# HGRN2 inside a hybrid trunk step: forward queries with backward keys in one tile, forward keys with backward queries in another, scaled over all 128 rows, with a PSUM bank and a mask per direction

## The chip, the cores and the metric

The kernel runs on one core of a Trainium2 chip. The metric is the device time of one execution in microseconds (us); lower is better. A profile of one execution lists each engine's instructions: PE (TensorE matmuls; PEld its weight loads), DVE (VectorE), ACT (ScalarE), POOL (GpSimd), and SP (SyncE, which issues most DMAs).

## What is computed

One inference step of a trunk of two layers over 640 tokens: 512 latent tokens (four tiles of 128, numbers 0 to 3) and 128 prompt tokens (tile 4). In each layer a modulation, one input projection, three token mixers side by side (differential attention, gated DeltaNet, HGRN2), one output projection, a layer norm and a SwiGLU feed-forward part. The change touches HGRN2, which has 4 heads of 64 keys and 64 values and scans the tokens in both directions:

```
def hgrn_mixer(q_raw, f_raw, i_raw, gate, lb, norm_g, s0):
    q = silu(q_raw)                                   # one set of queries for both directions
    v = i_raw
    forget = lbb + (1.0 - lbb) * sigmoid(f_raw)       # per direction, token, head and key
    key = 1.0 - forget
    g = log(forget)
    o_f, s_f = gla_chunked(q, key[0], v, g[0], s0[:, 0])
    o_b, s_b = gla_chunked(_flip(q), _flip(key[1]), _flip(v), _flip(g[1]), s0[:, 1])
    o = o_f + _flip(o_b)
    return rms_norm(o, norm_g) * silu(gate), [s_f, s_b]
```

`gla_chunked` is gated linear attention in pieces of the sequence (b is the cumulated sum of g inside a piece):

```
    dec = jnp.where(causal, jnp.exp(b_t - b_s), 0.0)
    attn = jnp.einsum('bhntsd,bhnsd->bhnts', q * dec, k)
    intra = jnp.einsum('bhnts,bhnse->bhnte', attn, v)
    o = intra_n + jnp.einsum('bhcd,bhde->bhce', q_n * jnp.exp(b), S)
    S = S * jnp.exp(b_last) + jnp.einsum('bhcd,bhce->bhde', k_n * jnp.exp(b_last - b), v_n)
```

So token t reads key s at or before it with the weight of q_t on key_s times the product of the forgets after s up to t, and the state that came in.

## The kernel before

Tokens are kept with the 64 keys of a head on the partitions: rows 0 to 63 belong to the forward direction, rows 64 to 127 to the backward one, and a tile is 128 rows x 4 heads x 128 tokens. `hgrn_local` makes the weights inside a tile by levels instead of by divisions of cumulated products. At level n (1, 2, 4, ... 64) the tile's tokens stand in pairs of blocks of n. A query in the later block of a pair (for the backward direction, the earlier one) reads the keys in the other block; its own product of forgets since its block's border is already multiplied into it, and into the keys the product up to the border. After a level, queries of the later blocks and keys of the earlier ones are multiplied by the whole product over the other block, which the tile `T` (names hT) holds for each block and which is itself halved by a product of neighbours (`Tn`).

The names and lines: `q5` (hq) holds the queries of all five tiles, loaded twice, into rows 0 to 63 and 64 to 127; `f5` (hf) the forgets of both directions; `Kr` (hK) a tile's keys of both directions. The local function `diag` makes 8 matmuls for a tile (4 heads, 2 halves of 64 tokens), each over all 128 rows, so that both directions are summed in one bank (names ph{level}_{layer}_{tile}). So that each direction brings only its own pairs, ACT first copies the half of the queries that may read (`A.copy`, L623) into a tile `Qm` (hqm) whose other positions POOL set to zero at the stage's start (L1443; nine tiles in layer 0, eight in layer 1). DVE takes the level's new weights out of the bank into `aD` (haD) where the level's mask is set (L624, `copy_predicated`); the mask hmask has 64 columns for each of six levels. Then DVE scales the queries and POOL the keys, two operations each, one for every direction's 64 rows (L176 is the line of the helper `tt` that issues all of them), and POOL makes Tn. At level 64 there are 8 matmuls of 64x64 without a mask. `key_T` transposes the keys (phk, hkn); pha are the tile's sums of keys and values, pho the outputs, pth their transposition into `xT`.

The PSUM banks are given out by classes: during this stage the class "h" of HGRN has three banks, P2, P2b and R2, which it takes in turn; "as" and "pt_po" belong to attention, "m" to the modulation.

What runs beside it: `open_h` (L1432) starts HGRN together with the modulation matmuls (`mods`, names psm) and with the output of DeltaNet; attention runs through the same time, one block per head and query tile (pas_{layer}_{head}_{tile} scores, anm, ae softmax, pat, pao, ao, asm, pto). Python generators are taken in turns (`run` with TURNS), and a scheduler sets the order in which each engine gets its instructions. After the stage the output projection (pop) fills PE. The mask and the attention's lambda (dl) are loaded at the program's start through SP's queue.

Of the kernel before, what the change touches and what calls it, by code (L numbers as in the profile page):

```python
# [10 lines left out]
F32 = mybir.dt.float32  # L11
# [34 lines left out]

NQ2 = (3, 2)
LATE = (2, 2)
# [6 lines left out]
def _const_arrays():  # L55
# [41 lines left out]
    for k, a in parts.items():  # L97
# [3 lines left out]
        cols.append(a)  # L101
    m = [((rc // (2 * b)) == (tc // (2 * b))) & ((rc // b) != (tc // b)) for b in (1, 2, 4, 8, 16, 32)]
    _CONST["f"] = np.concatenate(cols, 1)
# [6 lines left out]
def tile_trunk(  # L110
# [269 lines left out]

    hmask = cp.tile([P, 6 * 64], U8, name="hmask")
    hmf = cp.tile([P, 6 * 64], F32, tag="dl", name="hmf")
    S.dma_start(hmf, constm)
    V.tensor_copy(hmask, hmf)

# [192 lines left out]

    def hgrn_local(l, taus, hp, st, hqm, f5):
        X = {}  # L580
        q5 = hp.tile([P, 4, NTOK], F32, name=f"hq{l}")
        v5 = hp.tile([P, NT, 256], F32, name=f"hv{l}")
        for d in range(2):
            ds_ = slice(64 * d, 64 * d + 64)
            S.dma_start(q5[ds_], cqs[l].rearrange("(h j) t -> j h t", j=64))
        S.dma_start(v5, cis[l].rearrange("(t p) c -> p t c", p=P))
        for tau in taus:
            tsl = slice(tau * P, (tau + 1) * P)
            n_ = f"{l}_{tau}"
            q, f, v = q5[:, :, tsl], f5[:, :, tsl], v5[:, tau]  # L590
            Kr = hp.tile([P, 4, P], F32, tag="hK", bufs=NT, name=f"hK{n_}")
            T = hp.tile([P, 4, P], F32, tag="hT", bufs=NT, name=f"hT{n_}")
            aD = hp.tile([P, 4, 64], F32, tag="haD", bufs=NT, name=f"haD{n_}")
            X[tau] = dict(q=q, f=f, v=v, Q=q, K=Kr, T=T, aD=aD, Tv=f, To=0)

        def diag(x, rhs, nm):
            ps = psS("h", nm)
            pv = ps[:, :256].rearrange("p (h t) -> p h t", t=64)
            for h in range(4):
                for c_ in range(2):  # L600
                    cs = slice(64 * c_, 64 * c_ + 64)
                    mm(pv[cs, h, :], x["K"][:, h, cs], rhs[:, h, cs])
            return pv

        for tau in taus:
            x = X[tau]
            V.tensor_scalar(x["K"], x["f"], -1.0, 1.0, ALU.mult, ALU.add)
            tt(V, x["aD"], diag(x, x["q"], f"ph0_{l}_{tau}"), bc(K("identc"), 1, 4), ALU.mult)
            tt(G, x["Q"], x["q"], x["f"], ALU.mult)
        yield  # L610
        for i, n in enumerate((1, 2, 4, 8, 16, 32, 64)):
            nb = P // (2 * n)
            for tau in taus:
                x = X[tau]
                Q, Kr, T, Tv = x["Q"], x["K"], x["T"], x["Tv"]

                def half(ap, d, u):
                    return ap[64 * d:64 * d + 64].rearrange("p h (b u n) -> p h b u n", u=2, n=n)[:, :, :, u, :]

                if n < 64:  # L620
                    Qm = hqm[i][tau % len(hqm[i])]
                    for d in range(2):
                        A.copy(half(Qm, d, 1 - d), half(Q, d, 1 - d))  # L623
                    V.copy_predicated(x["aD"], bc(hmask[:, i * 64:(i + 1) * 64], 1, 4),  # L624
                                      diag(x, Qm, f"ph{n}_{l}_{tau}"))
                else:
                    aT = x["f"]
                    x["aT"] = aT
                    ps = psS("h", f"ph{n}_{l}_{tau}")
                    po = ps[:, :256].rearrange("p (h t) -> p h t", t=64)  # L630
                    for h in range(4):
                        for c_ in range(2):
                            cs, co = slice(64 * c_, 64 * c_ + 64), slice(64 - 64 * c_, 128 - 64 * c_)
                            mm(po[cs, h, :], Kr[cs, h, cs], Q[cs, h, co])
                    for c_ in range(2):
                        cs, co = slice(64 * c_, 64 * c_ + 64), slice(64 - 64 * c_, 128 - 64 * c_)
                        A.copy(aT[cs, :, cs], x["aD"][cs])
                        A.copy(aT[cs, :, co], po[cs])
                for d in range(2):
                    up, lo = 1 - d, d  # L640

                    def tb(u):
                        y = Tv[64 * d:64 * d + 64].rearrange("p h (b u) -> p h b u", u=2)[:, :, :, u]
                        return y.unsqueeze(3).to_broadcast([64, 4, nb, n])
# [4 lines left out]
                Tp = Tv.rearrange("p h (b u) -> p h b u", u=2)  # L649
                tt(G, Tn, Tp[:, :, :, 0], Tp[:, :, :, 1], ALU.mult)  # L650
                x["Tv"], x["To"] = Tn, x["To"] + nb
            yield

        def key_T(tau):
            ps = psS("h", f"phk{l}_{tau}")
            pk = ps.rearrange("p (j t) -> p j t", t=P)
            for h in range(4):
                nc.tensor.transpose(pk[:, h, :], X[tau]["K"][:, h, :], ident)
            kn = hp.tile([P, 4, P], F32, tag="hkn", bufs=2, name=f"hkn{l}_{tau}")
            A.copy(kn, pk)  # L660
            return kn

        kn = key_T(taus[0])
        for i, tau in enumerate(taus):
            x, nxt = X[tau], key_T(taus[i + 1]) if i + 1 < len(taus) else None
            ps = psS("h", f"pha{l}_{tau}")
            pa = ps[:, :256].rearrange("p (h v) -> p h v", v=64)
            for h in range(4):
                mm(pa[:, h, :], kn[:, h, :], x["v"][:, h * 64:h * 64 + 64])
            Ab = x["T"][:, :, 0:64]  # L670
            A.copy(Ab, pa)
            st[tau] = (x["Q"], x["Tv"][:, :, 0], Ab, x["aT"], x["v"])
            kn = nxt
# [15 lines left out]

    def hgrn(l, hp, hqm, xT, f5):  # L690
        ready = []
# [22 lines left out]

        yield from hgrn_local(l, list(range(NT)), hp, st, hqm, f5)
        for d in range(2):
# [628 lines left out]
    for l in range(DEPTH):  # L1345
# [86 lines left out]
        def open_h(rest):  # L1432
# [13 lines left out]
            return [(mods(), TURNS[l][3]), (hgrn(l, hp, hqm, xT, held["f5"]), TURNS[l][4]), (delta_T(), 1)]  # L1446

# [323 lines left out]
```

## Time and profile before

| | |
|---|---|
| median of 3 runs | 2097.5 us (2095.54 to 2103.86) |
| the profiled execution | 2094.8 us, span 2093.0 us |
| mean granted clock | 0.956 |
| busy, share of the span | PE 91%, PEld 80%, DVE 69%, ACT 38%, POOL 42% |
| HGRN levels, layer 0 | 379.5 to about 480 us |
| HGRN levels, layer 1 | about 1410 to 1510 us |

Shares of the span are means over stages with different limits. A row of a group of instructions gives its busy time, the mean of one, and the engine's idle time just before it with what ended it. The clock is TensorE's, in parts of full speed.

### The profile page before, as it was taken

The numbers are of one execution on the slowest core, as the hardware profiler recorded it, in microseconds if no ns is written. First come the engines' busy times: TensorE is split into PE (matmuls) and PEld (weight loads), VectorE is DVE, ScalarE is ACT, GpSimd is POOL, SyncE is SP. The second block draws the span as 40 slices with busy tenths as digits, with TensorE's granted clock in tenths as the row PEclk, the third lists the DMA queues.
The fourth block names the chain that finished last, engine by engine and source line by source line (L and its number), as shares of the span: only waits on it lengthen the run. The fifth ranks groups of instructions, "written<-read, shape, count | busy, mean of one in ns | idle before, by whom it ended". The sixth has DMA issues, their size and how long they took to land.

```text
span 2093.0 us, 37831 instructions
## 1 busy us (share of the span) xinstructions
PE 1912.6 (91%) x14914; PEld 1676.2 (80%) x14914; DVE 1439.1 (69%) x2516; ACT 792.7 (38%) x1564; POOL 883.5 (42%) x988
## 2 busy tenths in 40 slices
PE   7999997888978999999989999978889789999996
PEld 5988986667758989989989879755677779989895
DVE  5458524897488867667666774359847897667676
ACT  3542322666143334323345323146742434334231
POOL 0375235775042132444246814358632311432445
PEclk7999998898999999999999999989899899999998
DMA  8423225865453323222433331386344233223221
GB/s 282 132 77 122 90 68 140 218 195 196 146 164 94 109 81 101 68 84 76 127 121 109 123 116 56 101 192 201 125 158 135 83 109 91 71 81 101 71 77 75
DMA packets 243400, 249.36 MB, mean 119 GB/s; under 512 B 19371, under 2 KB 190359, under 8 KB 243223
## 3 DMA queue, kind: packets, MB, share of 16 engines
q1 hardware_dynamic: 240630, 245.11, 38.4%
q8 instruction: 118, 1.93, 0.4%
q10 hardware_dynamic: 2592, 1.84, 0.3%
q14 instruction: 60, 0.48, 0.1%
HBM read 218.72 MB, written 28.18 MB: 118 GB/s over the span
## 4 chain that ended last, share of the span: by engine, by line
PE 26%; DVE 10%; POOL 5%; DMA 3%; issue 3%; ACT 2%; SPq 1%; POOLq 0%; ACTq 0%; DVEq 0%
PE pfo L173 6%; PE pfd L173 3%; PE pfc L173 3%; PE pfa L173 3%; PE pop L173 3%; PE pfb L173 1%; PE pci L173 1%; DVE hl L176 1%; DVE hq L176 1%; PE pcf L173 1%; POOL r L176 1%; PE pbq L173 1%; PE ph L173 1%; DVE fs L176 1%; DMA avf<-vsc 1%
## 5 line engine op out<-in xcount | busy, mean ns | idle before, releaser
L176 DVE TENSOR_TENSOR hl<-raw,hl 128x1024 fp32r<-128x1024 f32 (+1 forms) x210 | 279.6, 1335 | 92.1 <-ACT hl L273 74.2
L173 PE MATMUL pfo<-hl,ha 128*128 128x512 f32 x1320 | 312.8, 395 | 1.6 <-ACT hl L273 0.8
L173 PEld LDWEIGHTS pfo<-hl,ha 128*128 128x128 f32 x1320 | 246.1, 187 | 60.6 <-DVE ha L176 1.6
L176 POOL TENSOR_TENSOR r<-r,ft 128x512 f32<-128x512 f32 x96 | 142.8, 1506 | 245.2 <-DVE ft L176 244.4
L176 POOL TENSOR_TENSOR t<-raw 128x512 f32<-128x512 f32 x44 | 65.7, 1493 | 336.6 <-DMA raw<-in_w_ffn_in_dram 168.3
L273 ACT CAST hl<-raw 128x1024 fp32r<-128x1024 f32 (+2 forms) x122 | 125.9, 1036 | 152.4 <-DMA raw<-in_w_ffn_out_dram 47.8
L173 PE MATMUL pfc<-sx,hl 128*128 128x320 f32 x1056 | 173.4, 312 | 9.8 <-ACT hl L1550 7.2
L173 PE MATMUL pfa<-xT,hl 128*128 128x320 f32 x1056 | 172.7, 313 | 4.7 <-DVE hl L176 3.0
L173 PEld LDWEIGHTS pfc<-sx,hl 128*128 128x128 f32 x1056 | 161.5, 190 | 13.5 <-ACT hl L1550 7.8
L1550 ACT CAST hl<-raw 128x1024 fp32r<-128x1024 f32 x88 | 92.0, 1051 | 204.4 <-PE pfo L173 105.7
L173 PEld LDWEIGHTS pfa<-xT,hl 128*128 128x128 f32 x1056 | 161.0, 191 | 8.0 <-DVE hl L176 3.8
L173 PE MATMUL paq<-xT,hl 128*128 128x320 f32 x768 | 123.8, 318 | 1.4 <-ACT az L1238 1.4
L173 PE MATMUL pop<-hl,xT 128*128 128x512 f32 x480 | 122.4, 407 | 0.0
L173 PEld LDWEIGHTS paq<-xT,hl 128*128 128x128 f32 x768 | 116.1, 191 | 4.5 <-ACT az L1238 2.1
L173 PEld LDWEIGHTS pop<-hl,xT 128*128 128x128 f32 x480 | 89.5, 193 | 25.2 <-issue 6.8
L176 DVE TENSOR_TENSOR ft<-pfo,lg 128x512 f32<-128x512 f32 x96 | 63.8, 683 | 54.6 <-PE pfo L173 44.1
L176 POOL TENSOR_TENSOR hK<-hK,hT 64x256 f32<-64x256 f32 x120 | 87.6, 730 | 29.9 <-PE ph L173 23.2
L176 DVE TENSOR_TENSOR t<-raw,t 128x512 f32<-128x512 f32 x88 | 73.9, 840 | 35.7 <-POOL t L176 35.6
L173 PE MATMUL pfd<-xT,h 128*128 128x320 f32 x528 | 85.2, 310 | 10.0 <-DVE u L176 10.0
L173 PE MATMUL pbq<-xT,hl 128*128 128x320 f32 x576 | 89.7, 312 | 1.0 <-DVE hl L176 0.4
L173 PE MATMUL pfb<-sx,hl 128*128 128x320 f32 x528 | 88.7, 310 | 0.6 <-DVE hl L176 0.6
L173 PEld LDWEIGHTS pfd<-xT,h 128*128 128x128 f32 x528 | 79.0, 188 | 11.6 <-issue 8.9
(409 smaller groups left out, 4206.1 us busy)
## 6 DMA issues: line engine op xcount, KB each, us to landing
raw<-in_w_ffn_in_dram SPq DMA_DIRECT2D x96, 512.0 KB
raw<-in_w_mod_dram SPq DMA_DIRECT2D x80, 512.0 KB
raw<-in_w_in_dram SPq DMA_DIRECT2D x56, 512.0 KB
raw<-in_w_ffn_out_dram SPq DMA_DIRECT2D x44, 512.0 KB
pc<-in_w_mod_dram SPq DMA_DIRECT2D x8, 1024.0 KB
raw<-in_w_out_dram SPq DMA_DIRECT2D x16, 512.0 KB
qksc<-az SPq DMA_DIRECT2D x16, 320.0 KB
qkhi<-azs SPq DMA_DIRECT2D x16, 256.0 KB
```

Source lines behind the costliest of these rows:

```text
L173: nc.tensor.matmul(out, lhsT, rhs, start=start, stop=stop, **kw)
L176: return eng.tensor_tensor(out, a, b, op)
L273: A.copy(hl[:, 0, :kt * n], raw[:, :kt * n])
L1550: A.copy(tile_[:, 0, :n], raw)
```

## The change

The queries and keys of a direction no longer stand in tiles of their own kind. `x5` (hx) holds the forward queries in rows 0 to 63 and the backward keys in rows 64 to 127; `y5` (hy) the forward keys and the backward queries. Of a pair of blocks the later one is scaled in x for both directions (forward queries, backward keys) and the earlier one in y, so each is one operation over 128 rows. x is scaled by DVE for even tiles and by POOL for odd ones, y always by POOL. The loads of queries go from two to three. Level 0 still uses a tile with both directions' keys (`kt`, names hk0), from which ACT copies the two halves into their places; the queries' first product is two POOL operations of 64 rows.

At levels 1 to 32 each direction has a bank of its own: 16 matmuls of 64x64 for a tile, two `copy_predicated` with a mask for each direction (12 masks of 64 columns, loaded in three parts through the buffer of dl). Qm, its copies and memsets go. `key_T` transposes x and y, copies the half of each that holds keys, and then puts the backward queries beside the forward ones.

```diff
-        for d in range(2):
-            S.dma_start(q5[ds_], cqs[l].rearrange("(h j) t -> j h t", j=64))
+        for sl, t5 in ((LO, x5), (HI, x5), (HI, y5)):
+            S.dma_start(t5[sl], cqs[l].rearrange("(h j) t -> j h t", j=64))
...
-            V.tensor_scalar(x["K"], x["f"], -1.0, 1.0, ALU.mult, ALU.add)
-            tt(V, x["aD"], diag(x, x["q"], f"ph0_{l}_{tau}"), bc(K("identc"), 1, 4), ALU.mult)
-            tt(G, x["Q"], x["q"], x["f"], ALU.mult)
+            kt = hp.tile([P, 4, P], F32, tag="hk0", bufs=2, name=f"hk0{l}_{tau}")
+            V.tensor_scalar(kt, f, -1.0, 1.0, ALU.mult, ALU.add)
...
+                    mm(pv[cs, h, :], kt[:, h, cs], x["x"][:, h, cs])
+            for k, sl in ((kf, LO), (kb, HI)):
+                A.copy(k, kt[sl])
+            tt(V, x["aD"], pv, bc(K("identc"), 1, 4), ALU.mult)
+            for q, sl in ((qf, LO), (qb, HI)):
+                tt(G, q, q, f[sl], ALU.mult)
...
                 if n < 64:
-                    Qm = hqm[i][tau % len(hqm[i])]
+                    pv = [psS("h", f"ph{n}_{d}_{l}_{tau}")[:, :256].rearrange("p (h t) -> p h t", t=64) for d in range(2)]
+                    for h, d, c_, cs in chunks():
+                        k, q = x["kq"][d]
+                        mm(pv[d][cs, h, :], k[:, h, cs], q[:, h, cs])
                     for d in range(2):
-                        A.copy(half(Qm, d, 1 - d), half(Q, d, 1 - d))
-                    V.copy_predicated(x["aD"], bc(hmask[:, i * 64:(i + 1) * 64], 1, 4),
-                                      diag(x, Qm, f"ph{n}_{l}_{tau}"))
+                        V.copy_predicated(x["aD"], bc(hmask[:, (2 * i + d) * 64:(2 * i + d + 1) * 64], 1, 4), pv[d])
...
-                for d in range(2):
-                    up, lo = 1 - d, d
...
-                    tt(V, half(Q, d, up), half(Q, d, up), tb(lo), ALU.mult)
-                    tt(G, half(Kr, d, lo), half(Kr, d, lo), tb(up), ALU.mult)
+                def scaled(eng, ap, u):
+                    y = ap.rearrange("p h (b u n) -> p h b u n", u=2, n=n)[:, :, :, u, :]
+                    tt(eng, y, y, Tp[:, :, :, 1 - u].unsqueeze(3).to_broadcast([P, 4, nb, n]), ALU.mult)
+
+                scaled(G if tau % 2 else V, x["x"], 1)
+                scaled(G, x["y"], 0)
...
+            for src, sl in ((x["y"], LO), (x["x"], HI)):
+                pk = psS("h", f"phk{sl.start}_{l}_{tau}").rearrange("p (j t) -> p j t", t=P)
                 for h in range(4):
+                    nc.tensor.transpose(pk[:, h, :], src[:, h, :], ident)
+                A.copy(kn[:, :, sl], pk[:, :, sl])
+            A.copy(x["x"][HI], x["y"][HI])
...
-            hqm = [[hp.tile([P, 4, P], F32, name=f"hqm{l}_{i}_{j}") for j in range(2 if i < NQ2[l] else 1)]
-                   for i in range(6)]
-            for t_ in hqm:
-                for q_ in t_:
-                    G.memset(q_, 0.0)
```

The scheduler's order shifts with it. DVE's instructions where level 8 of layer 0 begins, in the kernel before (ae, anm, ao and ari are attention's, with layer, head and tile in the name; ph8_0_2 is level 8, layer 0, tile 2; x2 marks two of a kind):

```order
L624 COPY_PREDICATED haD0_0_4296<-hmask_347,ph8_0_0_5022 128x256
L176 TENSOR_TENSOR hq0_4289<-hq0_4289,hT0_1_4298 64x4x8x8 x2
L1136 SCALAR_TENSOR_TENSOR ae0_1_p_0_4711<-ae0_1_p_1_4714,ari0_1_p_4716,ae0_1_p_0_4711 128x128
L624 COPY_PREDICATED haD0_1_4299<-hmask_347,ph8_0_1_5039 128x256
L176 TENSOR_TENSOR hq0_4289<-hq0_4289,hT0_2_4301 64x4x8x8 x2
L1125 TENSOR_REDUCE anm0_2_0_4749<-pas0_2_0_1_4744 128x1
L624 COPY_PREDICATED haD0_2_4302<-hmask_347,ph8_0_2_5056 128x256
L1108 SCALAR_TENSOR_TENSOR ao0_1_2_4409<-ao0_1_2_4409,asm0_1_2_4407,dn0_384 128x128
L176 TENSOR_TENSOR hq0_4289<-hq0_4289,hT0_3_4304 64x4x8x8 x2
L1134 RECIPROCAL ari0_2_0_4757<-ar0_2_0_4750 128x1
L624 COPY_PREDICATED haD0_3_4305<-hmask_347,ph8_0_3_5073 128x256
L1135 SCALAR_TENSOR_TENSOR ari0_2_0_4757<-ar0_2_0_4750,nlam0_381,ari0_2_0_4757 128x1
```

The same place in the changed kernel (ph8_1_0_2 is direction 1, layer 0, tile 2; xT are the transposed outputs):

```order
L636 COPY_PREDICATED haD0_0_4285<-hmask_347,ph8_0_0_0_5115 128x256
L178 TENSOR_TENSOR hx0_4277<-hx0_4277,hT0_0_4284 128x4x8x8
L636 COPY_PREDICATED haD0_0_4285<-hmask_347,ph8_1_0_0_5116 128x256
L1119 SCALAR_TENSOR_TENSOR ao0_2_0_4843<-ao0_2_0_4843,asm0_2_0_4841,dn0_390 128x128
L636 COPY_PREDICATED haD0_1_4287<-hmask_347,ph8_0_0_1_5138 128x256
L636 COPY_PREDICATED haD0_1_4287<-hmask_347,ph8_1_0_1_5139 128x256
L636 COPY_PREDICATED haD0_2_4289<-hmask_347,ph8_0_0_2_5161 128x256
L178 TENSOR_TENSOR xT1_4134<-pto0_1_4_1_5048,xT1_4134 128x128
L636 COPY_PREDICATED haD0_2_4289<-hmask_347,ph8_1_0_2_5162 128x256
L178 TENSOR_TENSOR hx0_4277<-hx0_4277,hT0_2_4288 128x4x8x8
L636 COPY_PREDICATED haD0_3_4291<-hmask_347,ph8_0_0_3_5184 128x256
L1119 SCALAR_TENSOR_TENSOR ao0_2_1_5041<-ao0_2_1_5041,asm0_2_1_5039,dn0_390 128x128
```

A tile's two hq operations of 64 partitions (x2) have become one hx operation of 128 for tiles 0, 2 and 4 and none for 1 and 3, and there are two haD rows for each tile. The attention beside them moved too: before, the block whose ao stands here is head 1's tile 2; now it is head 2's tile 0.

PE's instructions at the end of level 64 in layer 0, before (ph64_0_4 is tile 4 at level 64, psm the modulation, pas0_3_0 the first attention block of head 3):

```order
L173 MATMUL psm1_1_5516<-raw_5535,cm_84 32x256 x4
L1206 MATMUL pao0_2_3_5301<-c_ident_82,ae0_2_3_0_5291 128x128
L173 MATMUL ph64_0_4_5613<-hq0_4289,hK0_4_4306 64x64 x7
L658 MATMUL phk0_1_5716<-c_ident_82,hK0_1_4297 128x128 x4
L173 MATMUL psm1_1_5516<-raw_5681,cm_84 32x256 x4
L658 MATMUL phk0_0_5709<-c_ident_82,hK0_0_4294 128x128 x4
L173 MATMUL pas0_3_0_0_5464<-aks_4958,aqs_4957 128x320 x4
L1206 MATMUL pao0_2_2_5133<-c_ident_82,ae0_2_2_0_5123 128x128
L173 MATMUL psm1_1_5516<-raw_5687,cm_84 32x256 x4
```

And in the changed kernel:

```order
L175 MATMUL ph64_0_4_5790<-hy0_4278,hx0_4277 64x64
L669 MATMUL phk0_0_0_5885<-c_ident_82,hy0_4278 128x128 x4
L669 MATMUL phk64_0_0_5891<-c_ident_82,hx0_4277 128x128 x4
L175 MATMUL pas0_3_1_1_5811<-aks_5053,aqs_5052 128x320
L175 MATMUL pas0_3_1_1_5811<-aqs_5052 128x320
```

Before, the last ph64 stands ahead of the first scores of head 3's first block (pas0_3_0_0); now it stands behind them and the first half of the second block's scores, whose second half (pas0_3_1_1) follows.

## Rows read from the trace of the kernel before

**Rows 1.** The page's first part: busy us (share of the span) x instructions.

```profile
PE 1912.6 (91%) x14914; PEld 1676.2 (80%) x14914; DVE 1439.1 (69%) x2516; ACT 792.7 (38%) x1564; POOL 883.5 (42%) x988
```

**Rows 2.** Busy time by stretches: us from:to, length, each engine (PE, PEld, DVE...).

```profile
core 0: us, PE busy (x) PEld busy (x) DVE busy (x) ACT busy (x) POOL busy (x), PEclk, DMA share, GB/s
380.00:400.00 20.00, 15.23 (x185) 11.25 (x180) 17.54 (x37) 13.70 (x41) 18.28 (x33) 0.89 0.79 241
380.00:480.00 100.00, 85.27 (x1088) 59.18 (x1083) 93.35 (x203) 64.84 (x195) 79.24 (x125) 0.90 0.66 207
480.00:524.00 44.00, 36.75 (x294) 32.56 (x291) 32.31 (x73) 27.50 (x79) 22.17 (x34) 0.93 0.57 192
1410.00:1510.00 100.00, 81.47 (x1022) 59.16 (x1022) 90.28 (x193) 63.85 (x186) 75.47 (x111) 0.87 0.57 180
1510.00:1551.00 41.00, 32.84 (x242) 29.38 (x240) 28.75 (x69) 23.70 (x78) 21.52 (x36) 0.94 0.14 40
```

**Rows 3.** Timeline of layer 0, at three places: start us, us, engine, line.

```profile
379.48 1.15 PE L173 MATMUL ph<-hq,hK 128*64 128x64 f32 x32 [1.11 <-DMA hq<-cqs]
...
403.00 0.69 PE L173 MATMUL ph<-hqm,hK 128*64 128x64 f32 x16
...
524.41 1.91 PE L173 MATMUL pop<-hl,xT 128*128 128x512 f32 x5
```

**Rows 4.** Waits of 355 to 500 us: total us, times, longest us.

```profile
POOL asm L1106 <- ACT ajk L1104: 17.9, 7, 8.4
ACT ae L1131 <- DVE anm L1125: 17.3, 14, 7.5
POOL hK L176 <- PE ph L173: 12.0, 12, 3.3
ACT hqm L623 <- PE ph L173: 10.3, 9, 5.0
...
POOL hT L176 <- DMA hf<-cfs: 5.0, 1, 5.0
```

**Rows 5.** DVE's groups by shape, 355 to 500 us: busy us, mean ns.

```profile
L176 DVE TENSOR_TENSOR hq<-hq,hT 64x256 f32<-64x256 f32 x60 | 34.4, 577 | 1.2 <-ACT hqm L623 0.2
...
L176 DVE TENSOR_TENSOR hq<-hq,hf 64x256 f32<-64x256 f32 x10 | 7.1, 709 | 0.2
...
L624 DVE COPY_PREDICATED haD<-hmask,ph 128x256 f32<-128x256 uint8 x30 | 12.8, 438 | 0.2
...
L1125 DVE TENSOR_REDUCE anm<-pas 128x1 f32<-128x640 f32 x26 | 21.3, 818 | 7.7 <-PE pas L173 7.3
...
L1136 DVE SCALAR_TENSOR_TENSOR ae<-ae,ari,ae 128x640 f32<-128x640 f32 x14 | 13.3, 947 | 0.1
...
L1108 DVE SCALAR_TENSOR_TENSOR ao<-ao,asm,dn 128x128 f32<-128x128 f32 x12 | 7.0, 582 | 0.9 <-POOL asm L176 0.8
```

**Rows 6.** POOL's groups by shape in the same stretch.

```profile
L176 POOL TENSOR_TENSOR hK<-hK,hT 64x256 f32<-64x256 f32 x60 | 43.4, 723 | 11.8 <-PE ph L173 8.7
L176 POOL TENSOR_TENSOR hK<-hK,hf 64x256 f32<-64x256 f32 x10 | 9.9, 991 | 3.8 <-PE ph L173 3.3
L176 POOL TENSOR_TENSOR hq<-hq,hf 128x512 f32<-128x512 f32 x5 | 7.5, 1505 | 2.0 <-PE ph L173 2.0
...
L1443 POOL MEMSET hqm<- 128x512 f32 x9 | 4.2, 524 | 0.1
...
L176 POOL TENSOR_TENSOR hT<-hf 128x256 f32<-128x256 f32 x5 | 3.9, 815 | 5.0 <-DMA hf<-cfs 5.0
```

**Rows 7.** The tile hq, whole span: ns min/median/max, first and last start.

```profile
L176 DVE TENSOR_TENSOR hq<-hq,hT x120: 397/423/1365, 387.8 to 1511.1; 64x256 f32<-64x256 f32 x120
```

**Rows 8.** ACT's groups by shape, 355 to 500 us.

```profile
L623 ACT COPY hqm<-hq 64x256 f32<-64x256 f32 x60 | 24.0, 410 | 13.5 <-PE ph L173 10.3 <-DVE hq L176 2.5
```

**Rows 9.** Timeline of SP's queue at the program's start.

```profile
41.43 0.38 SPq L420 DMA_DIRECT2D dl<-in_diff_lambda_dram  x1
...
47.61 1.67 SPq L420 DMA_DIRECT2D dl<-in_diff_lambda_dram  x1
```

More of the change, by code (lines that the diff above doesn't have):

```diff
@@ L101, in _const_arrays @@
         cols.append(a)
-    m = [((rc // (2 * b)) == (tc // (2 * b))) & ((rc // b) != (tc // b)) for b in (1, 2, 4, 8, 16, 32)]
+    m = []
+    for b in (1, 2, 4, 8, 16, 32):
+        blk = (rc // (2 * b)) == (tc // (2 * b))
+        m += [blk & (rc // b < tc // b), blk & (rc // b > tc // b)]
     _CONST["f"] = np.concatenate(cols, 1)
@@ L379, in tile_trunk @@
     close(ic)
[L381 to L384, printed above, removed]
+    hmask = cp.tile([P, 12 * 64], U8, name="hmask")
+    for i in range(3):
+        cs_ = slice(256 * i, 256 * i + 256)
+        hmf = cp.tile([P, 256], F32, tag="dl", name=f"hmf{i}")
+        S.dma_start(hmf, constm[:, cs_])
+        V.tensor_copy(hmask[:, cs_], hmf)
     lbx = pcol[:, 36:44].rearrange("p (d l b) -> p d l b", d=2, l=DEPTH)
@@ L575, in ln_last, with hgrn_local @@
         S.dma_start(dst[:, :n], r[:, :n])
-    def hgrn_local(l, taus, hp, st, hqm, f5):
+    def hgrn_local(l, taus, hp, st, f5):
         X = {}
-        q5 = hp.tile([P, 4, NTOK], F32, name=f"hq{l}")
+        x5 = hp.tile([P, 4, NTOK], F32, name=f"hx{l}")
+        y5 = hp.tile([P, 4, NTOK], F32, name=f"hy{l}")
         v5 = hp.tile([P, NT, 256], F32, name=f"hv{l}")
-        for d in range(2):
-            ds_ = slice(64 * d, 64 * d + 64)
-            S.dma_start(q5[ds_], cqs[l].rearrange("(h j) t -> j h t", j=64))
+        LO, HI = slice(0, 64), slice(64, 128)
+        for sl, t5 in ((LO, x5), (HI, x5), (HI, y5)):
+            S.dma_start(t5[sl], cqs[l].rearrange("(h j) t -> j h t", j=64))
         S.dma_start(v5, cis[l].rearrange("(t p) c -> p t c", p=P))
@@ L654, in key_T @@
         def key_T(tau):
[L655 to L658, printed above, removed]
+            x = X[tau]
             kn = hp.tile([P, 4, P], F32, tag="hkn", bufs=2, name=f"hkn{l}_{tau}")
-            A.copy(kn, pk)
+            for src, sl in ((x["y"], LO), (x["x"], HI)):
+                pk = psS("h", f"phk{sl.start}_{l}_{tau}").rearrange("p (j t) -> p j t", t=P)
+                for h in range(4):
+                    nc.tensor.transpose(pk[:, h, :], src[:, h, :], ident)
+                A.copy(kn[:, :, sl], pk[:, :, sl])
+            A.copy(x["x"][HI], x["y"][HI])
             return kn
@@ L671, in hgrn_local @@
             A.copy(Ab, pa)
[L672 removed]
+            st[tau] = (x["x"], x["Tv"][:, :, 0], Ab, x["aT"], x["v"])
             kn = nxt
@@ L688, in head_norm_out, with hgrn @@
         return o.rearrange("p h d -> p (h d)")
-    def hgrn(l, hp, hqm, xT, f5):
+    def hgrn(l, hp, xT, f5):
         ready = []
@@ L713, in turn @@
                 to_T(o, xT, tau, f"pth{l}_{tau}", ((6, 8),), 6, "h")
-        yield from hgrn_local(l, list(range(NT)), hp, st, hqm, f5)
+        yield from hgrn_local(l, list(range(NT)), hp, st, f5)
         for d in range(2):
```

38 lines of the change are left out of this document (17 added, 21 removed).

## The prediction, before the run

> **What bounds the kernel now.** I read the page's first part, then the busy time of each engine by stretches, then the waits and the costliest groups of the stretch that the change touches. Over the whole span TensorE is busy 91% [rows 1], so most stages can only shrink with PE's work. The HGRN levels are the exception. They run beside the attention blocks and the modulation matmuls, in layer 0 from the first ph matmul at 379.48 to about 480 us [rows 3] and in layer 1 from 1410 to 1510. There DVE is busy 93.4 and 90.3 us of 100, PE only 85.3 and 81.5, POOL 79.2 and 75.5, ACT 65 and 64 [rows 2]. In the waits of 355 to 500 us the long ones are POOL behind the attention's ACT, ACT behind DVE's anm, and hK and hqm behind PE's ph [rows 4]: a ring of HGRN and attention in which DVE is the fullest engine. After it, up to the first pop matmul at 524.41 [rows 3], comes a tail in which no engine is full (PE 36.8 of 44 us; 32.8 of 41 in layer 1) [rows 2]. So time saved by the change has to come out of the two level stretches, and there by way of DVE, less so of PE's 14.7 and 18.5 us of idle time, which a chain through several engines makes.
>
> **DVE in the level stretch.** Each tile and level scaled queries twice with 64 rows: 60 operations with hT at 0.577 us (34.4) and 10 with hf at 0.709 (7.1) per layer, 41.5 us in all [rows 5]. They go. Added are 128-row x scalings of the even tiles, 3 tiles by 7 levels. No row shows a 64x256 and a 128x256 product on DVE side by side. On POOL they stand close: 0.723 us for hK with 64 rows, 0.815 for hT with 128 [rows 6]. I therefore take the 64-row price: 3 x 0.709 + 18 x 0.577 = 12.5 us. The uncontended median of hq, 0.423 us [rows 7], bounds it below at 8.9; twice the price, 25.0, bounds it above. copy_predicated goes from 30 to 60 a layer, each still 128x256 out of PSUM: 30 x 0.438 = 13.1 us [rows 5]. The first product (kt) stays on DVE with its shape. Sum: 12.5 + 13.1 - 41.5 = -15.9 us of DVE work per layer.
>
> Not all of it shortens the stretch. In the order of the PE two more attention blocks stand ahead of the last level than before, and a block brings DVE two anm (0.818), one ae (0.947) and one ao (0.582) [rows 5]: 3.2 us; with its reciprocal, subtraction and transposed copies I estimate 3.9, so +7.8. Net -8.1 us, and at DVE's busy share of 0.934 the stretch shortens by 8.7 us. That the blocks are taken out of the tail pays little there, because its PE is not full and its length is set by chains: I count -1 for them and the longer key transposition together.
>
> In these rows the hq scalings have a median of 0.423 us over both layers, a maximum of 1.365 [rows 7] and a mean of 0.577 beside POOL's hK in layer 0 [rows 5]. The Trainium skill, "SBUF — State Buffer", section "SBUF: two separate sides", says why: a DVE operation with two SBUF inputs and a GpSimd operation that reads SBUF hold one pair of ports in turn, each for its whole instruction; the spread agrees. By that rule fewer such pairs would bring x near 0.423 and the sum some 7 us further down over both layers; I keep the mean of the rows.
>
> **POOL.** Per layer hK's 60 + 10 operations (43.4 + 9.9 us) become 35 y scalings of 128 rows, and the odd tiles' x add 14: 42 x 0.723 + 7 x 0.991 = 37.3, so -16 us at the 64-row price [rows 6] (-12 at 0.815). But the start of the stretch gets heavier: the product of queries with hf is split by rows, 10 of 64x512 where there were 5 of 128x512 at 1.505 [rows 6]: +7.5 us if a half costs what a whole does, as I take it by the 64-row and 128-row prices above, 0 if it costs half. The first level's scalings give back 9.9 - 7 x 0.991 = 3.0. In 380 to 400 us POOL is busy 18.3 of 20 us [rows 2], so this would be on the path; since DVE and PE have other work queued there, I take half of 4.5: +2.3 per layer. The bounds are 0 and +4.5. The memsets (9 x 0.524 [rows 6]) go; they stand where POOL waits 5.0 us for hf to land anyway [rows 4], so taking them out gives nothing; without that wait it would give 4.7.
>
> **ACT.** 60 hqm copies go (24.0 us); 10 copies of kt and two more copies per tile at the keys' transposition, at the same 0.41 each [rows 8], bring about 8 back: -16 us on an engine busy 65 of 100. I cost it at nothing by itself; what it takes out of the chain is that ph waits no more for hqm, 10.3 us of ACT waiting for PE [rows 4] being the other side of the same hand-over.
>
> **PE.** A level and tile has 16 matmuls of 64x64 instead of 8 of 128x64. Eight are 16 records that take 0.69 us, 32 records take 1.15 [rows 3]: 0.46 us more for 16 records, by 30 pairs 14 us per layer, if they run one behind another. If the four quadrants run at the same time it is 0. Even at 14 it fits the PE's idle time of 14.7 and 18.5 us, which hides it as long as PE is not what the others wait for; where that cover is gone it costs up to 14 per layer. I take 0. The trace has no group of matmuls in four quadrants, so this stays open. The Trainium skill, "TensorEngine Tiling (Array Packing)", section "Tiling Modes", says that tiles load weights and multiply in parallel, by which the term would be 0, but also that a change of the tiling mode drains the array, which a mixed order of ph, pas and psm would pay each time; no row here shows that price.
>
> **Start.** The mask's DMA becomes three through the buffer of dl, and dl's own two move behind weight loads on SP's queue (41.43 and 47.61 us now [rows 9]). Two more issues at 0.4 to 1.7 us each [rows 9] make 0.8 to 3.4 on a queue that feeds the weights; I put this at +2 (0 to 4).
>
> **Sum.** 2 x (-8.7 + 2.3 - 1.0) + 2 = -12.8 us, against the profiled execution's 2094.8: 2082. The median of the runs is 2.7 above that execution, so 2084.7, or 2085. Half a per cent, 10.5 us, is about what a measurement of this kernel can tell from no change; the sum passes it by little.
>
> **Rivals.**
> *No change, 0.28.* The relief is refilled: DVE's freed time goes to attention blocks that stand before a tail that ends no sooner, because HGRN's own chain (levels, keys' transposition, states, output) now ends last before pop. For it: the tail's engines are not full [rows 2]. Then the 8.7 us are worth 0 to 4 a layer and the ramp and the start take them: 2 x (-4 + 2.3 - 1) + 2 = -3 to 2 x 2.3 + 2 = +7, 2094 to 2104, say 2098.
> *Slower by the banks, 0.15.* This ends on the other side. The class of PSUM banks for HGRN keeps three. Before, a tile's level took one and PE could run three tiles ahead of DVE; now a tile takes two, so PE stands a tile and a half ahead and must wait until copy_predicated of direction 0 of the tile before has read its bank. Behind that wait on PE's queue stand attention and modulation matmuls, for which ACT and DVE wait in turn. A wait is a copy (0.44) with an attention operation ahead of it (0.82 [rows 5]), up to 1.25 us, at 30 pairs a layer and 60 in all. At 0.2 us a pair it eats the gain (12 us); from 0.4 it makes the kernel slower by more than half a per cent (24 - 12.8); at 0.5 the time is 2115. Against it: PE has other work in between, and DVE has less queued.
> *PE doubles and its cover is gone, inside "no change".* With half of 14 us per layer on the path: 2085 + 14 = 2099.
> *It does not do what it says, 0.05.* If a 128-row operation costs two of 64 rows, DVE loses another 12.5 us per layer of its gain and only 3.4 are left, less than the moved blocks bring: 2 x (4.7 + 2.3 - 1) + 2 = +14, 2111. The rows 0.723 and 0.815 speak against.
>
> **How the numbers follow.** The forecast has 0.52, with its own range 2070 to 2091: low, x at 0.423 (-3.6 / 0.934 = -3.9 a layer), no ramp (-2.3 a layer) and no start (-2); high, the full ramp (+2.2 a layer) and start (+2). The whole range starts at 2062, where in one layer the moved blocks cost nothing either (-8.4), and takes in no change and the nearer half of the slower cases, to 2113. Faster by over 0.5% (under 2087) has 0.49, the forecast less its upper end; within 0.31; slower (over 2108) 0.20.
>
> **What would show it.** In the level stretches: x on DVE near 0.58 us with 128 rows, copy_predicated 60 times at 0.44, DVE's share below 93%, and the stretch 6 to 9 us shorter per layer. POOL's 64x512 products near 1.5 us, not 0.75. 32 records of ph in about 0.7 us if quadrants overlap, 1.15 if not. Waits of PE's ph for DVE haD above some 12 us over both layers would mean the bank rival. The forecast is wrong if the stretch is as long as before with DVE at 80% or less: then the chain, not DVE, was the bound.

## The result, and the profile after

The changed kernel takes 2116.1 us (median of 11 runs, 2104.4 to 2120.5) against 2097.5 before; the ratio is 1.0078, 95% interval 1.0059 to 1.0097, so it is slower by 12 to 20 us. I had forecast 2085. The profiled execution is 2107.4 us with a span of 2105.6, so it lies at the low end of its runs. The page's first part for it:

```profile
PE 1958.3 (93%) x15914; PEld 1722.5 (82%) x15914; DVE 1410.4 (67%) x2480; ACT 770.4 (37%) x1488; POOL 849.1 (40%) x939
```

DVE, ACT and POOL have 29, 22 and 34 us less to do than in [rows 1]; PE has 46 us and 1000 records more. By stretches, with the columns of [rows 2] (the levels of layer 0 run from 385.7 to 497.5 us, those of layer 1 from 1408.8 to 1527.8):

```profile
385.00:485.00 100.00, 95.07 (x1432) 69.88 (x1432) 76.02 (x180) 43.81 (x139) 57.65 (x96) 0.93 0.70 212
385.70:497.50 111.80, 107.13 (x1647) 78.05 (x1648) 87.21 (x200) 53.67 (x164) 67.14 (x111) 0.94 0.68 208
498.00:536.00 38.00, 33.36 (x243) 31.28 (x241) 24.81 (x57) 25.59 (x79) 17.42 (x27) 0.85 0.31 97
1408.80:1527.80 119.00, 108.44 (x1582) 81.04 (x1583) 87.48 (x197) 52.11 (x160) 68.36 (x116) 0.87 0.57 172
```

The order of the busy engines has turned over. In 100 us of levels DVE fell from 93.4 to 76.0, ACT from 65 to 44, POOL from 79 to 58, and PE rose from 85.3 to 95.1 [rows 2]. In layer 0 the stretch grew from 99 to 112 us. The tail to the first pop, which stands at 536.2, is 7 us shorter (38.7 against 46.1), because attention has gone further by then.

In layer 1 the stretch grew from 98 to 119 us, but there the length misleads: it holds attention that stood ahead of the levels or in the tail before (76 score matmuls instead of 56; the tail is 34 us instead of 43). From that layer's projection pbg, which begins at 1068.4 us (1056.3 before), to its first pop at 1562.0 (1551.1) both kernels take 494 us. Of the 12.6 us between the two spans, 6 are lost at the start and 6 in layer 0.

The single operations came out as they were costed, but for ACT's copies of 64x512. DVE, then POOL, then one of ACT's copies, groups by shape, 361 to 515 us (busy us, mean ns, idle before):

```profile
L636 DVE COPY_PREDICATED haD<-hmask,ph 128x256 f32<-128x256 uint8 x60 | 25.8, 441 | 7.9 <-PE ph L175 7.4
...
L178 DVE TENSOR_TENSOR hx<-hx,hT 128x256 f32<-128x256 f32 x18 | 10.0, 560 | 0.0
```

```profile
L178 POOL TENSOR_TENSOR hy<-hy,hT 128x256 f32<-128x256 f32 x30 | 21.8, 731 | 11.8 <-PE ph L175 11.7
L178 POOL TENSOR_TENSOR hx<-hx,hT 128x256 f32<-128x256 f32 x12 | 8.5, 711 | 9.9 <-PE ph L175 9.9
...
L178 POOL TENSOR_TENSOR hy<-hy,hf 64x512 f32<-64x512 f32 x5 | 6.6, 1345 | 0.1
L178 POOL TENSOR_TENSOR hx<-hx,hf 64x512 f32<-64x512 f32 x5 | 6.3, 1267 | 3.4 <-PE ph L175 3.3
```

```profile
L620 ACT COPY hx<-hk 64x512 f32<-64x512 f32 x5 | 3.1, 616 | 6.0 <-PE ph L175 5.9
```

128 rows cost what 64 did (0.56 for 0.577, 0.73 for 0.723), copy_predicated 0.441. What DVE and POOL wait for is now PE's ph. In the waits of that stretch POOL's scalings alone wait 27 us for it, where hK waited 12.0 before [rows 4] (total us, times, longest):

```profile
POOL hx L178 <- PE ph L175: 13.7, 10, 3.0
POOL hy L178 <- PE ph L175: 13.6, 12, 2.9
...
DVE haD L636 <- PE ph L175: 7.4, 12, 1.1
```

The other loss is at the start. The projection pbq of layer 0 ends at 121.3 us instead of 115.2, and everything up to the levels lies 6 us later. The timeline there (SP issues lambda's second part, ACT works on its first part, gate activations follow):

```profile
58.84 0.34 SPq L424 DMA_DIRECT2D dl<-in_diff_lambda_dram  x1
58.84 0.29 DVE L429 TENSOR_REDUCE dls<-dlp 128x2 f32<-128x128 f32 x1
59.16 0.20 ACT L430 ACTIVATE dls<-dls 128x2 f32<-128x2 f32 x1 [4.90 <-DVE dls L429]
...
59.28 5.84 SPq L1255 DMA_DIRECT2D gsc<-gt  x2
...
62.29 1.28 ACT L1253 ACT_TABLE_LOAD   x1 [2.61 <-DMA gsc<-gt]
...
63.59 0.38 ACT L1253 ACTIVATE gt<-pbg 128x256 f32<-128x256 f32 x1
63.99 1.28 ACT L430 ACT_TABLE_LOAD   x1
64.00 0.24 DVE L1282 COPY bb<-pbg 128x8 f32<-128x8 f32 x2 [1.34 <-ACT gt L1253]
...
64.39 1.02 PE L175 MATMUL pbg<-hl,xT 128*128 128x272 f32 x3 [3.45 <-DVE bb L1282]
```

Lambda's load stands behind the mask's (dl was issued at 41.43 us before [rows 9]), ACT waits 4.9 us for its exponential with a gate activation queued behind it, the gate frees PE's bank late, and PE stands 3.45 us. Two more things hold that gate up. Its buffer is emptied by the DMA gsc, whose issue stands behind lambda's second load on SP's queue (58.84, then 59.28); that is a wait of 2.61 us. And exponentials and gates now take turns on ACT, which loads an activation table each time it changes from one to the other: five loads of 1.28 us between 49 and 68 us, where the kernel before, with both exponentials done ahead of the first gate, has one.

### The profile page after: what moved, and what is told of

It reads as the page before. It is cut to its first block, busy times and chain, and to the rows that moved or that the text cites. A ratio compares the mean times of both kernels' runs of the same rounds, so it can differ in the third digit from the quotient of the medians.

```text
span 2105.6 us, 39680 instructions
## 1 busy us (share of the span) xinstructions
PE 1958.3 (93%) x15914; PEld 1722.5 (82%) x15914; DVE 1410.4 (67%) x2480; ACT 770.4 (37%) x1488; POOL 849.1 (40%) x939
## 3 DMA queue, kind: packets, MB, share of 16 engines
q1 hardware_dynamic: 241462, 246.62, 38.7%
## 5 line engine op out<-in xcount | busy, mean ns | idle before, releaser
L175 PE MATMUL pfa<-xT,hl 128*128 128x320 f32 x1056 | 177.1, 318 | 7.1 <-DVE ms L178 3.1
L175 PEld LDWEIGHTS pbq<-xT,hl 128*128 128x128 f32 x576 | 86.6, 191 | 4.6 <-ACT hl L275 1.8
```

Source lines behind the costliest of these rows:

```text
L175: nc.tensor.matmul(out, lhsT, rhs, start=start, stop=stop, **kw)
```

## The experiments

Theory: PE's added records are not hidden, they set the level stretch. Rivals: the banks (PE's lead over copy_predicated), the start, or the chain of DVE and POOL. Each run was timed against the kernel before on its own chip (medians there 2094.2 to 2096.0); ratios are against that. In every version the scheduler orders the instructions anew, so an edit also moves attention against the levels; a few us between two versions can be that.

**The changed kernel again.** No edit.

> The changed kernel once more, unaltered, for a second profile on the chip that the next three run on. Its 11 runs so far spread from 2104 to 2120 us, and the profiled one (2107.4) lies at the lower end. Both theories of the level stretch (PE full, or PE held up by banks) expect 2104 to 2120 again; if the profile is of an execution near 2117 it should show where the other 10 us go: the start stage (pbq ends at 121 us in the profile, 6.1 later than before), the stretch of levels, or TensorE's granted clock.

2120.0 us, ratio 1.0101 (1.0083 to 1.0120). The profile is of an execution of 2123.3 us, 16 us longer than the first one, and 12 of these are in one place, the levels of layer 0:

```profile
386.60:510.30 123.70, 117.76 (x1647) 83.40 (x1647) 87.94 (x200) 53.38 (x163) 66.54 (x111) 0.86 0.62 185
```

The same 1647 records take 118 us of PE at a mean granted clock of 0.86, and 107 at 0.94 in the first profile. Length times clock is 106 and 105 us: with PE full, time spent at the lower of its two levels (1.2 against 2.4 GHz) is lost to the kernel.

**8 matmuls, and 16 in one bank.**

```diff
-                    for h, d, c_, cs in chunks():
-                        k, q = x["kq"][d]
-                        mm(pv[d][cs, h, :], k[:, h, cs], q[:, h, cs])
+                    pw = psS("h", f"ph{n}_{l}_{tau}")[:, :256].rearrange("p (h t) -> p h t", t=64)
+                    pv = [pw, pw]
+                    for h in range(4):
+                        for c_ in range(2):
+                            cs = slice(64 * c_, 64 * c_ + 64)
+                            mm(pw[cs, h, :], x["y"][:, h, cs], x["x"][:, h, cs])
```

The second kernel issues these matmuls twice.

> The changed kernel with 8 matmuls over 128 rows into one bank for a tile and level instead of 16 of 64x64 into two, both copies reading that bank (so the two directions are mixed and the weights are not the reference's). DVE, ACT and POOL keep all their work. If PE's extra records or the banks are what the change lost, the stretch of levels in layer 0 falls from 112 us to 90 to 98 and the time by 15 to 30 us in all, to about 2090. If DVE, POOL or the chains between them set the stretch, it stays within 3 us of 112 and the time does not fall.

> As the run with 8 matmuls, but these 8 are issued twice into the same bank, so PE has 32 records for a tile and level as in the changed kernel while only one of three banks is used for it. If PE's records are the cost, the stretch stays at 108 to 114 us and the time within 5 us of the changed kernel. If the two banks are the cost (PE only a tile and a half ahead), it falls nearly as far as the run with 8, to 90 to 100 us.

With 8: 2082.3 us, ratio 0.9930 (0.9914 to 0.9946). With 16 into the same bank: 2108.9, 1.0054 (1.0033 to 1.0076); once more on another chip 2109.2, 1.0059 (1.0042 to 1.0076).

> The run with 8 matmuls issued twice into one bank once more, beside the next on the same chip: 2105 to 2113 as before.

Nothing but PE's records, and the order that the scheduler makes with them, lies between the two kernels: 1.24%, 26 us, 13 a layer on average. The level stretches, first with 8, then with 16:

```profile
388.50:484.90 96.40, 87.17 (x1090) 61.57 (x1094) 76.98 (x181) 44.80 (x138) 63.20 (x101) 0.90 0.73 217
1410.60:1496.90 86.30, 74.45 (x1007) 53.67 (x1008) 73.06 (x174) 41.69 (x126) 62.27 (x87) 0.94 0.72 213
```

```profile
387.90:498.70 110.80, 107.17 (x1606) 80.52 (x1610) 82.65 (x191) 49.81 (x155) 63.20 (x106) 0.94 0.65 194
1431.10:1524.30 93.20, 87.24 (x1488) 68.92 (x1488) 77.06 (x173) 43.05 (x130) 62.16 (x87) 0.96 0.63 192
```

And the kernel with 8, which has all that the change does to DVE, ACT and POOL, stands 3 us from the 2085 that I forecast with PE at nothing; how far that agreement goes is said below.

**The kernel before with its level matmuls issued twice.** In `diag`, `for u_ in range(2):` around the loops, for levels 1 to 32.

> The kernel before with the matmuls of levels 1 to 32 issued twice into the same bank, so PE has 32 records a tile and level there too, beside all the DVE, ACT and POOL work of before. My prediction held that 14 us a layer would be hidden in PE's 15 to 19 us of idle time while DVE bounds the stretch: then at most +8, to 2105. If that idle time is no cover (PE's work delays the engines that wait for it, one by one), +20 to +28, to 2116 to 2124.

2114.9 us, 1.0098 (1.0080 to 1.0116): 20 us more, 10 a layer, so they are not hidden beside a DVE that is the fullest engine either. The level stretches (the profiled execution, 2123.7 us, is the slowest of the five):

```profile
383.80:505.60 121.80, 112.74 (x1678) 83.95 (x1678) 104.43 (x222) 75.95 (x226) 83.40 (x132) 0.97 0.62 193
1425.40:1539.10 113.70, 95.73 (x1526) 74.08 (x1526) 91.97 (x201) 66.09 (x197) 72.72 (x111) 0.95 0.49 149
```

They grew by 23 and 16 us, but they also took in attention: the tails shrank from 46 and 43 us to 25 and 34. Marks that attention does not move across give each layer's cost without that (us, one profiled execution each; by the changed kernel's two, the middle column can move by 16 us with the clock):

| profiled execution | to the end of pbq, layer 0 | from there to layer 1's pbg | from there to layer 1's first pop |
|---|---|---|---|
| before | 115.2 | 941.1 | 494.8 |
| before, matmuls twice | 117.3 | 952.6 | 503.2 |
| changed | 121.3 | 947.1 | 493.6 |
| changed, again | 120.1 | 962.7 | 494.5 |
| changed, 8 matmuls | 120.3 | 938.6 | 481.4 |
| changed, 16 in one bank | 122.7 | 950.8 | 491.7 |

The doubled records cost 12 and 8 us in the kernel before, and 12 and 10 between the runs with 8 and 16. In layer 1's levels PE stays idle for 18 of 114 us, as for 18 of 98 before, and the layer is still longer. That fits idle time which is waiting in a chain, where work put on a link lengthens the chain; the chain itself was not taken apart.

**The kernel before with 14 DVE operations a layer on POOL.**

```diff
-                    tt(V, half(Q, d, up), half(Q, d, up), tb(lo), ALU.mult)
+                    tt(G if d and tau % 2 else V, half(Q, d, up), half(Q, d, up), tb(lo), ALU.mult)
```

> The kernel before with the backward queries' scalings of tiles 1 and 3 on POOL instead of DVE: 14 operations a layer, 8.1 us of DVE at 0.577, some 10 us more on POOL (0.723 each), PE untouched. If DVE bounds the level stretch, as the prediction held, the stretch falls by 5 to 8 us a layer and the time by 5 to 15, to 2081 to 2091. If POOL, then 88 to 90% busy, or the chain through the engines is as tight, within 4 us of before.

2094.8 us, 0.9993 (0.9980 to 1.0007). DVE fell from 92 to 87 us in layer 0's stretch and nothing came of it, POOL being at 86 by then. So DVE's share alone did not make the time. Whether POOL, up from 78 us, had become the bound, and whether the gain of the run with 8 matmuls needed DVE, POOL and ACT to fall together, is not shown.

**The mask's loads.** In the kernel before, the mask in three parts through dl's buffer; in the changed one, a buffer of its own (`tag="hmf"`).

> The kernel before with its mask loaded in three parts through dl's buffer, so that lambda's loads stand behind them as in the changed kernel. Theory of the start: PE loses 3 to 4 us to the wait for bb and about as much after it, pbq ends at 120 to 122 us instead of 115, and the time rises by 5 to 7 us, to 2101 to 2103. Rival (the start's loss comes from elsewhere in the change, or is caught up later): within 2 us of before.

> The changed kernel with a buffer of its own for the mask's three parts, so that lambda's loads no longer stand behind them. Theory of the start (lambda's load comes later, ACT waits for its exponentials between the gates' activations, and PE waits for both): pbq ends 5 to 6 us earlier, at 115 to 116 us, everything after it moves up, and the time falls by 5 to 6 us against the changed kernel on this chip. Rival (the 6 us are of the weight loads behind the mask's DMAs on the same queue): no change, pbq ends at 120 to 121.

In the kernel before it costs 4.4 us: 2099.7, 1.0021 (1.0010 to 1.0032), and its profile has pbq end at 119.0, with the same five table loads on ACT. In the changed kernel the own buffer gives 2110.2, 1.0075 (1.0055 to 1.0094), against 1.0101 beside it, with overlapping intervals; ACT is back to one table load and PE's wait for bb is gone, but pbq still ends at 119.9, at a lower granted clock from 100 to 120 us (0.74 against 0.91). The sign is shown; the size in the changed kernel is not, since the order of attention moves too (pas begins 7 us earlier).

**Half the columns.** Only queries that may read go through PE, 32 columns a matmul, and copy_predicated takes these alone.

```diff
-                        mm(pv[d][cs, h, :], k[:, h, cs], q[:, h, cs])
+                        mm(pv[d][cs, h, :32], k[:, h, cs],
+                           q[:, h, cs].rearrange("p (b u n) -> p b u n", u=2, n=n)[:, :, 1 - d, :])
...
```

> The changed kernel with only the query columns that may read at a level as the matmul's moving operand: 64x64 keys by 32 queries, strided, and copy_predicated over these 128 of 256 columns a tile. The weights are complete. If a record's time goes by its columns, 32 records fall from 0.95 to about 0.5 us, PE gets the 13 us a layer back and DVE's copies shrink to about 0.3 us: the stretch of layer 0 comes to 90 to 98 us and the time to 2075 to 2090, below before. If a record takes 30 ns by its weight load whatever the columns, PE stays full and the time stays at 2105 to 2118.

2123.3 us, 1.0134 (1.0106 to 1.0162). DVE's 60 copies of layer 0 fell to 0.346 us, 7 us less, and that bought nothing: by the ratios it is 7 to 12 us slower than the changed kernel, 5 of them in its profile at the start, where nothing was edited. A record does not go by its columns (timeline, eight of one direction):

```profile
419.56 0.42 PE L175 MATMUL ph<-hy,hx 64*64 64x32 f32 x8
```

The last of these lasts 0.22, so the eight start within 0.20 us: 29 ns apart at 32 columns. Inside the runs of one direction four steps take 117 ns (median) in this trace and in the changed kernel's alike, so half the columns save nothing.

**Banks.** 16 matmuls over 128 rows, 8 into each of two banks (run twice); then two banks for HGRN instead of three (`"h": PP2`), in the kernel before, twice, and in the changed one, without and with the mask's own buffer.

> The changed kernel with 16 matmuls over 128 rows, 8 into each of its two banks (directions mixed, so the weights are not the reference's). It has the two banks a tile of the changed kernel, and PE's number of records, but no 64x64 quadrants. The run with 16 into one bank stood at 2109, the changed kernel at 2120 on that chip. If the second bank costs those 11 us (PE only a tile and a half ahead), this is at 2115 to 2122; if the quadrants or the order that comes with them cost it, at 2105 to 2111.

> The run with 16 matmuls over 128 rows into two banks once more. If the second bank costs PE its lead, 6 us or more above the one-bank run beside it; if not, within 3 us.

> The kernel before with two PSUM banks for HGRN instead of three, nothing else: PE can stand two tiles ahead of copy_predicated instead of three (one and a half in the changed kernel). It prices the bank rival without PE's records. If banks cost what is left of the changed kernel's loss (some 6 to 11 us), 2101 to 2107; if DVE's queue covers the shorter lead, within 3 us of before.

> The changed kernel with two banks for HGRN instead of three, so that PE can stand only one tile ahead of copy_predicated. The kernel before gained 16 us by the same edit. If a short lead in banks costs the changed kernel anything, it gets slower here, by 5 us or more, to above 2123. If fewer banks help by letting attention go first (in PE's order head 3's third and fourth block now stand ahead of the last level), it gains 5 to 16 us, to 2101 to 2113, with a shorter tail before pop. If PE's records alone set the stretch, it stays within 4 us of the changed kernel.

> The same with the mask's own buffer as well: 4 to 10 us below the run beside it, as the mask's run stood to the changed kernel. With both effects good, 2095 to 2105; it still has PE's records and should not come below the kernel before by more than 2 us.

> The kernel before with two banks once more, on this chip: 2077 to 2083, the fastest version so far that computes all; its two level stretches are 95 and 107 us as the runs before showed, the tails 42 and 21.

Two banks of 128-row matmuls: 2109.8 and 2111.4, 1.0083 (1.0057 to 1.0110) and 1.0067 (1.0047 to 1.0087), 2 to 6 us above one bank, with overlapping intervals. The changed kernel with a tile's lead only: 2126.5, 1.0161 (1.0126 to 1.0196), 12 to 17 us slower by the ratios; with the mask's buffer 2113.7, 1.0094 (1.0066 to 1.0122), against 1.0075 with three banks, not resolved. That it is PE's lead that costs is not shown: PE's ph waits for haD no longer than with three banks (PE 2.6 against 2.7 us in all), while the order moved, so that the end of layer 0's HGRN runs among the pop matmuls, which take 84 us instead of 66. The kernel before went the other way, to neither of the outcomes that I had written down: 2079.8, 0.9916 (0.9897 to 0.9935), and 2079.6, 0.9927 (0.9909 to 0.9946). The second run's stretches and tails:

```profile
381.70:477.50 95.80, 81.12 (x1106) 57.33 (x1110) 92.45 (x196) 64.02 (x192) 75.47 (x121) 0.95 0.71 224
477.50:520.90 43.40, 38.02 (x286) 34.86 (x286) 34.90 (x78) 28.32 (x85) 25.56 (x37) 0.89 0.28 84
1404.00:1509.20 105.20, 85.65 (x1028) 61.45 (x1028) 92.68 (x198) 65.96 (x193) 72.12 (x104) 0.83 0.52 163
1509.20:1529.90 20.70, 17.11 (x131) 15.95 (x129) 16.42 (x34) 15.25 (x44) 10.31 (x18) 0.92 0.06 18
```

Levels and tail together are 265 us against 285 of before (98.8 + 46.1 + 97.9 + 42.6 by the same marks). In layer 1 two more attention blocks stand ahead of the last level in PE's order, and the tail halves. One edit of a resource, 16 us: that is as large as what the change was about. That the order, not the banks themselves, brings it is argued, not shown.

**The banks crossed.** One bank takes (forward, tokens 0 to 63) and (backward, tokens 64 to 127), the other the rest; masks to match.

```diff
-                for d in range(2):
-                    for c_ in range(2):
-                        yield h, d, c_, slice(64 * c_, 64 * c_ + 64)
+                for g_ in range(2):
+                    for d in range(2):
+                        c_ = d ^ g_
+                        yield h, d, g_, slice(64 * c_, 64 * c_ + 64)
...
-                        mm(pv[d][cs, h, :], k[:, h, cs], q[:, h, cs])
+                        mm(pv[g_][cs, h, :], k[:, h, cs], q[:, h, cs])
```

> The changed kernel with the banks crossed: one bank takes the forward weights of tokens 0 to 63 and the backward ones of tokens 64 to 127, the other bank the other two, with masks made to match; all weights are complete. In the profiles so far 64x64 records that alternate between the two row halves follow each other in 15.6 to 20 ns, those of one direction alone in 31, and two thirds of them run one direction alone because the second bank comes free later. Here each bank has both row halves in it. If that is why PE's term came out at 13 us a layer, most runs of ph go at 16 to 20 ns, the term halves or better, and the time falls by 12 to 22 us against the changed kernel, to 2096 to 2106. If the pairing of rows has no such effect or the stretch is held by something else, it stays at 2110 to 2120.

> The same with the mask's own buffer: 4 to 12 us below the run beside it. With PE's term gone and the start mended it should come out as the run with 8 matmuls less the start, 2076 to 2096, below the kernel before; if the overlap does not come, 2104 to 2112 as the mask's run alone.

> The crossed banks and the mask's own buffer with two banks for HGRN instead of three. Two banks gained 16 us in the kernel before and lost 6 to 10 in the changed one. If they lost there because each tile's matmuls ran one direction at a time, the loss is gone here: 2070 to 2092, at or below the run beside it. If PE's lead over copy_predicated is what counts, 5 to 10 us above it.

2103.8 us, 1.0035 (1.0023 to 1.0048), the fastest of the changed family that computes all, and 9 to 14 us below it by the ratios; with the mask's buffer 2109.5, 1.0063 (1.0050 to 1.0076), with that and two banks 2110.4, 1.0063 (1.0049 to 1.0077). The reason that I gave for it fell. In the changed kernel's timeline, a run in which all four quadrants take turns (first and last rows; 24 records start within 0.35 us), and one of a single direction (16 records):

```profile
418.84 0.27 PE L175 MATMUL ph<-hx,hy 64*64 64x64 f32 x2
418.85 0.27 PE L175 MATMUL ph<-hy,hx 64*64 64x64 f32 x2
...
419.19 0.23 PE L175 MATMUL ph<-hy,hx 64*64 64x64 f32 x2
```

```profile
428.10 0.68 PE L175 MATMUL ph<-hx,hy 64*64 64x64 f32 x16
```

The first goes at 15 to 16 ns a record, the second at 31 ((0.68 - 0.22) / 15). With the banks crossed, a run of one bank, in which the two row halves do alternate (16 records, first and last rows):

```profile
499.12 0.27 PE L177 MATMUL ph<-hx,hy 64*64 64x64 f32 x1
499.13 0.27 PE L177 MATMUL ph<-hy,hx 64*64 64x64 f32 x1
...
499.58 0.22 PE L177 MATMUL ph<-hx,hy 64*64 64x64 f32 x1
499.58 0.22 PE L177 MATMUL ph<-hy,hx 64*64 64x64 f32 x1
```

Still 0.46 us for 15 steps, 31 ns. So it is not the pairing of row halves: two quadrants in turn go at 31 ns, the two column halves of one direction as well as the two on a diagonal, as two halves of columns did before (16 records in 0.69 us [rows 3]), and only four in turn go at half that. The starts of ph's records came closer in sum by some 5 us over both layers against the two profiles of the changed kernel; the rest of the 9 to 14 us is order and clock, not told apart. And the mask's own buffer, which looked like a gain beside the changed kernel, is a loss of 6 us here: a warning against summing such edits.

## Why the prediction was wrong

**The step that failed** is PE's term: "Even at 14 it fits the PE's idle time of 14.7 and 18.5 us, which hides it as long as PE is not what the others wait for ... I take 0." The bound was right, 14 us a layer; 13 were measured (8 against 16 matmuls), 10 in the kernel before. What was wrong is the cover. Its condition already failed in the rows of the kernel before, where POOL waited 12.0 and ACT 10.3 us for PE's ph [rows 4]. And idle time of an engine that others wait for was not free to be filled: in the kernel before the doubled matmuls cost 12 and 8 us by layers though PE kept 9 and 18 us idle in the stretches. I had written that PE's idle time is made by a chain through several engines, and then used it as cover all the same. The rival "PE doubles and its cover is gone" had the mechanism and half its price. The prediction's own sign of being wrong came: a stretch at least as long as before (112 us against 99) with DVE at 78%.

**DVE and POOL** were sized rightly: 128-row operations at the 64-row price, copy_predicated at 0.441, POOL's split products at 12.9 us against 15 costed, DVE's share at 76%. ACT's new copies take 12.5 us a layer, not 8, because those of 64x512 cost 0.61 and not the 0.41 of 64x256. With PE's records taken out the change gives 2082, where the sum had 2085. That agreement is in good part luck. The sum had 7.4 us in each layer and lost 2 at the start; by the table above that run gains 2.5 in layer 0 and 13.4 in layer 1 and loses 5 at the start. And the reason behind it, that DVE bounds the stretch, was too narrow: 5 us off DVE onto POOL gave nothing. The Trainium skill, "SBUF — State Buffer", section "SBUF: two separate sides", says that a DVE operation with two SBUF inputs and a GpSimd operation that reads SBUF hold one pair of ports in turn. By that rule the prediction would have had x near 0.423 with fewer POOL operations beside it; the mean of 0.560, and the median of 0.468 over both layers, do not bear that price out here.

**The start** was put at +2 and is +4.4 where it was measured alone; the mechanism was not the issue time but ACT, which waits for lambda's load with the gates behind it and loads a table at each change between exponential and gate.

**The quadrants.** The Trainium skill, "TensorEngine Tiling (Array Packing)", section "Tiling Modes", says that tiles load weights and multiply in parallel. The trace agrees in part: four quadrants in turn halve the spacing to 15.6 ns, by which the term would be nearly 0. The kernel gets there only in part, because much of its order runs one direction alone; that this is so because its two banks come free one after the other is argued. Between the starts inside runs of ph lie 62.5 us over both layers in the first profile, 42.2 with 8 matmuls and 70.8 with 16 of 128 rows: the quadrants gave back 8 of 29 us.

**The bank rival** did not come by the sign that the prediction gave for it, more than 12 us of PE's ph waiting for haD. Before and then changed, the whole span (PEld are PE's weight loads):

```profile
PE ph L173 <- DVE haD L624: 3.7, 3, 1.6
```

```profile
PEld ph L175 <- DVE haD L636: 4.1, 10, 0.8
...
PE ph L175 <- DVE haD L636: 2.7, 4, 1.1
```

Two banks with 128-row matmuls cost 2 to 6 us, not resolved. Two banks in all cost the changed kernel 12 to 17, whether by the shorter lead or by the moved order is not shown; with the banks crossed they cost nothing.

The balance by ratios: -15 us for the run with 8 matmuls (the start's +4 in it), +26 for PE's records, and the changed kernel's +16 to +21. Some 5 to 10 us stay unaccounted for, among banks, order and clock. If the changed kernel's records cost less than the 128-row ones in the measure of their starts (20 of 29 us, so an estimate of 18 instead of 26), it is 13 to 18.

## What to carry to other kernels

A layout that lets one vector operation serve 128 rows can split the matmul's contraction; count the records that this adds, and cost them in full unless another engine is shown to end last at every step. Test a cover by adding the work to the old kernel: one run with doubled matmuls would have told it. Where a scheduler decides, try the cheap resources (banks for a class, one more, one less) by themselves: the kernel before with one bank less, 2079.7 us, beats both.

## What the runs showed of the hardware

Matmul records of 64x64 f32 follow each other in 15.6 ns when all four quadrants take turns, in 31 when two do (two column halves, or a diagonal pair), and with half the columns no faster: inside a run of one direction four steps take 117 ns at 64 columns and at 32. An activation table takes ACT 1.28 us to load, at each change between exponential and gate. A stretch in which PE is 95% busy took 112 us at a mean granted clock of 0.94 and 124 at 0.86 in two executions of one program, with the same records; runs of the changed kernel spread over 16 us where those of the kernel before spread over 10. Why the clock was lower in the second was not found out. Not tried: a pair of banks that comes free as one, so that four quadrants always take turns.
